# A gated MLP as nine equal Strassen products instead of three wide and twelve narrow ones

## The chip, the cores and the metric

The kernel runs on one core of one Trainium2 chip. The metric is device microseconds from launch to the last output byte, median of the runs. A core has a matrix engine (PE, TensorE, whose weight loads are listed as PEld), a vector engine (DVE), an activation engine (ACT), GpSimd (POOL) and a queue engine (SP) that issues most of the DMA transfers.

## The reference, cut to what matters

The program is a two-layer decoder trunk on 256 tokens of width 1024, float32 throughout: attention, a mixture of experts, the gated MLP of this case, and a second mixture of experts. Each of the four adds its result to `ALPHA * x` and normalises. The gated MLP is:

```
z = gelu(x @ w_in + b_in)              # x 256x1024, w_in 1024x6144
u, v = split(z, 2)                     # 256x3072 each
v = layer_norm(v, ln_v_g, ln_v_b)      # over all 3072 columns
mixed = tril(w_s)[g] @ v[chunk, :, g]  + b_s[g]   # 8 groups of 384 columns; chunks of 128 tokens
h = (u * mixed) @ w_out                # w_out 3072x1024
x = layer_norm(ALPHA * x + h)
```

The 256 tokens make two chunks of 128 rows, called row tile 0 and 1 below.

## The kernel before, in words

All weights pass through a ring of 24 buffers of 1 MB in SBUF, each 128 partitions by 2048 floats (`slot`, `drop`, L68 to L76). `piece` (L78) takes a buffer and issues its load on SP's queue. SP works through its loads in order; a load starts when its buffer has been released, so transfers run ahead of the compute as far as the ring has free buffers. The ring also holds activations. The order of instructions on each engine is drawn up when the program is built, by a planner that follows the order of the code but takes a later instruction of the same engine first when, by its own reckoning, the earlier one's inputs are not there yet. On the chip each engine then works through that list in order.

Strassen's scheme (in Winograd's form) multiplies two matrices that are cut into 2x2 blocks with seven block products instead of eight, at the price of sums of blocks made beforehand and of results. Here a block product with 512 inner values is four matmul calls of 128 inner values each (`prod`, `prod_u`), and every float32 matmul call appears in the trace as two MATMUL instructions.

`gmlp` (L362) has these stages.

- **v**, L404 to L442: three passes of 1024 columns. The tokens are the stationary operand, 512 weight columns move; seven products of four matmuls each. The block sums of the weights are `t1`, `t2` and two sums in place: three on DVE and one, `b12 = b22 - b12`, on POOL (L422). The sums of x (`sums_x`, L354) are made once. DVE adds bias and partial results, ACT applies gelu, DVE takes the statistics of the layer norm.
- **u**, L483 to L519: twelve passes of 256 columns. Here the weights are the stationary operand and 128 tokens move (`prod_u`, L476), so that u comes out transposed, with columns in partitions. The sums of the weights are on DVE (`sums_w`, L448).
- **mix**, L525 to L548, inside the same loop: per 128 columns, `w_s` times the normalised v (L538), then bias, affine and the product with u on DVE (L534 to L546).
- **output projection**, `proj` (L471): 24 steps of 128 inner values, each with two row tiles times two halves of 512 columns, into four PSUM banks kept open through the whole loop. Its matmuls are placed between the products of the next u pass (`step`, L492).
- **close** (L211, called at L558 and L561): adds `ALPHA * x`, normalises each row tile and transposes it for the router of the second mixture of experts.

Before `gmlp`, at the end of the first mixture of experts, loads for its biases and `w_s` are issued from ACT's queue, behind the last block's Silu (`end = mid(pa, h)`, L904; `after(end)`, L369 and L388). PE's fillers `keep_warm(2)` (L903 and L920) multiply a matrix of ones. After `gmlp`, `moe(1, ...)` starts with the dense expert (`dense_up`, L593), the router (L578), and the first gather (L705).

Of the kernel before, what the change touches and what calls it, by code (L numbers as in the profile page):

```python
# [19 lines left out]
P = 128  # L20
# [29 lines left out]
def trunk(ctx: ExitStack, tc: tile.TileContext, t, out):  # L50
# [15 lines left out]
    held = {}  # L66

    def slot(late=False):  # L68
        i = idle.pop() if late else idle.popleft()
        s = ring.tile([P, 2048], F32, tag=f"s{i}", name=f"s{i}")  # L70
        held[id(s)] = (i, s)
        return s

    def drop(*slots):
        for s in slots:
            idle.append(held.pop(id(s))[0])  # L76
# [158 lines left out]

    def attention(xT_slot, x):
        xT = by_k(xT_slot)
        with tc.tile_pool(name="att", bufs=1) as att, tc.tile_pool(name="att2", bufs=2) as att2:
# [76 lines left out]
            for g in range(3):  # L315
                qkv_g = qkv(g, w)
                if g == 0:
                    nc.sync.dma_start(x, t["x"].rearrange("(a p) d -> p a d", p=P))
                w = [piece(t["wqkv"][3 * (g + 1) + i]) for i in range(3)]
                for c in range(2):  # L320
                    heads(g, c, *qkv_g, psY, "Y")
# [32 lines left out]
    def sums_x(xT, s):  # L354
        x11, x12, x21, x22 = (xT[:, 4 * h:4 * h + 4, a * P:(a + 1) * P] for a in range(2) for h in range(2))
# [3 lines left out]
        nc.vector.tensor_tensor(s[:, 2], x11, x21, op=OP.subtract)  # L359


    def gmlp(xT_slot, x, end):  # L362
        xT = by_k(xT_slot)
        with tc.tile_pool(name="gm", bufs=1) as gm, tc.tile_pool(name="gm2", bufs=2) as gm2:
            cols = gm.tile([P, 3, NCH], F32, name="cols")
            wb_slot = slot()
            wb = wb_slot.rearrange("p (i g q) -> p i g q", i=2, g=GG)
            ws, bs = wb[:, 0], wb[:, 1]
            with after(end):  # L369
                nc.scalar.dma_start(cols, t["gcols"])  # L370
                nc.scalar.dma_start(ws, t["gw_s"])
                nc.scalar.dma_start(bs, row_bc(t["gb_s"], GG * P).rearrange("p (g q) -> p g q", g=GG))
            nc.gpsimd.affine_select(out=ws, in_=ws, compare_op=OP.is_ge, fill=0.0, base=0,
                                    pattern=[[0, GG], [1, P]], channel_multiplier=-1)
            scr = gm.tile([P, 4 * T], F32, name="scr")
            b_slot = slot()
            s_slot = slot()
            sx = s_slot.rearrange("p (s k t) -> p s k t", s=4, k=4)
            x11, x12, x21, x22 = (xT[:, 4 * h:4 * h + 4, a * P:(a + 1) * P] for a in range(2) for h in range(2))
            s1, s2, s3, s4 = (sx[:, i] for i in range(4))  # L380
            v_slots, vt = [], []
            st = gm.tile([P, NT, 6, 6], F32, name="vst")

            def pair_load(p):
                w = [piece(t["wv"][4 * p + i]) for i in range(4)]
                bv = [b_slot[:, (2 * p + i) % 4 * 512:(2 * p + i) % 4 * 512 + 512] for i in range(2)]
                for i in range(2):
                    with after(end):  # L388
                        nc.scalar.dma_start(bv[i], row_bc(t["gb_v"][(2 * p + i) * 512:(2 * p + i + 1) * 512], 512))
                return w, bv  # L390

            def prod(ps, xs, w, start, stop):
                for k in range(4):
                    nc.tensor.matmul(ps, xs[:, k, :], by_k4(w)[:, k, :], start=start and k == 0, stop=stop and k == 3,  # L394
                                     skip_group_check=True)

            def add(o, i, j):
                nc.vector.tensor_tensor(o, i, j, op=OP.add)

            def sub(o, i, j, eng=nc.vector):  # L400
                eng.tensor_tensor(o, i, j, op=OP.subtract)  # L401


            ld = pair_load(0)  # L404
            for p in range(3):
                (b11, b21, b12, b22), bv = ld
                v_slots.append(slot(p > 0))
                vt.append(by_a(v_slots[-1]))
                c = [[vt[p][:, a, n * 512:(n + 1) * 512] for n in range(2)] for a in range(2)]
                t1, t2 = slot(True), slot(True)  # L410
                px, py, pz = bank(psA, "A"), bank(psY, "Y"), bank(psY, "Y")
                sub(t1, b12, b11)
                sub(t2, b22, t1)
                prod(px, x11, b11, True, False)
                prod(py, x12, b21, True, True)
                add(c[0][0], px, bv[0])
                if p == 0:
                    sums_x(xT, sx)
                add(c[0][0], c[0][0], py)
                prod(px, s2, t2, False, False)  # L420
                add(c[0][1], px, bv[1])
                sub(b12, b22, b12, nc.gpsimd)  # L422
                prod(pz, s1, t1, True, False)
                p5 = scr[:, p % 2 * 512:p % 2 * 512 + 512]
                nc.scalar.copy(p5, pz)
                drop(b11)
                sub(b21, b21, t2)
                prod(px, s3, b12, False, False)
                add(c[1][1], px, bv[1])
                prod(pz, s4, b22, False, True)  # L430
                add(c[0][1], c[0][1], pz)
                add(c[1][1], c[1][1], p5)
                nc.scalar.activation(vt[p][:, 0, :], vt[p][:, 0, :], AF.Gelu)
                if p < 2:
                    ld = pair_load(p + 1)
                prod(px, x22, b21, False, True)
                add(c[1][0], px, bv[0])
                nc.scalar.activation(vt[p][:, 1, :], vt[p][:, 1, :], AF.Gelu)
                for a in range(NT):
                    for n in range(2):  # L440
                        nc.vector.bn_stats(st[:, a, 2 * p + n, :], c[a][n])
                drop(b21, b12, b22, t1, t2)  # L442

            t_slots = [slot(True), slot(True)]
            wu = [piece(t["wu"][0])]


            def sums_w(q):  # L448
                w = by_k(wu[q])
                s = t_slots[q % 2].rearrange("p (s k n) -> p s k n", s=4, k=4)  # L450
                b11, b12, b21, b22 = (w[:, 4 * h:4 * h + 4, j * P:(j + 1) * P] for h in range(2) for j in range(2))
                sub(s[:, 0], b12, b11)
                sub(s[:, 1], b22, s[:, 0])
                sub(s[:, 2], b22, b12)
                sub(s[:, 3], b21, s[:, 1])
                return b11, b21, b22, s

            sw = sums_w(0)
            nrm = []
            for a in range(NT):  # L460
                mv = small.tile([P, 2], F32, tag="mv", name="mv")
                nc.vector.bn_aggr(mv, st[:, a])
                nrm.append((mv, rsqrt(mv[:, 1:2])))
            for cb in range(6):
                for a in range(NT):
                    v = vt[cb // 2][:, a, (cb % 2) * 512:(cb % 2) * 512 + 512]
                    nc.vector.tensor_scalar(v, v, nrm[a][0][:, 0:1], nrm[a][1], op0=OP.subtract, op1=OP.mult)

            acc = [[bank(psY, "Y") for _ in range(2)] for _ in range(NT)]

            def proj(a, i, mx, wo):  # L471
                for h in range(2):
                    nc.tensor.matmul(acc[a][h], mx[:, a, :], by_c(wo)[:, i % 2, h * 512:(h + 1) * 512],  # L473
                                     start=(i == 0), stop=(i == NCH - 1))

            def prod_u(ps, w, xs, start, stop):  # L476
                for k in range(4):
                    nc.tensor.matmul(ps, w[:, k, :], xs[:, k, :], start=start and k == 0, stop=stop and k == 3,  # L478
                                     skip_group_check=True)


            done = []
            for q in range(NCH // 2):  # L483
                wo = piece(t["wout"][q])
                if q + 1 < NCH // 2:
                    wu.append(piece(t["wu"][q + 1]))
                b11, b21, b22, tw = sw
                fill = [(a, *d) for d in done[-2:] for a in range(NT)]
                if q == NCH // 2 - 1:
                    fill = [f for f in fill if f[0] == 0]  # L490

                def step():  # L492
                    if fill:
                        proj(*fill.pop(0))

                px, py, pz = (bank(psA, "A")[:, :P], bank(psB, "B")[:, :P], bank(psB, "B")[:, :P])
                u = [gm2.tile([P, T], F32, tag="u", name="u", bufs=3) for _ in range(2)]
                p5 = gm.tile([P, P], F32, tag="p5", name="p5")
                prod_u(px, b11, x11, True, False)
# [493 lines left out]
```

## Time and profile before

| what | value |
|---|---|
| median of 3 runs (lowest to highest) | 1350.84 us (1348.72 to 1351.52) |
| the profiled execution: time of its own | 1352.34 us |
| its span, first to last instruction | 1350.6 us |
| PE busy | 1234.4 us (91%), 6706 matmuls |
| DVE busy | 346.9 us (26%) |
| ACT busy | 133.5 us (10%) |
| DMA | 469.05 MB, mean 347 GB/s |

The page cuts the span into 40 slices of 33.8 us. The gated MLP lies in slices 19 to 26 of them (618.9 to 874.1 us). In the two mixtures of experts the DMA line stands at 9 and some 420 GB/s; in the gated MLP the DMA moves 149 to 277 GB/s in most slices. "Busy" of PE is the time in which at least one matmul is in flight; the rate of matmuls is read from the distance between their starts.

### The profile page before, as it was taken

The page shows a single profiled execution, that of the slowest core. Times are in us where ns is not written, and L with a number is a line of the kernel's source. Part 1 is how long each engine was busy: PE and PEld are TensorE (multiplying, and loading weights), DVE is VectorE, ACT ScalarE, POOL GpSimd, SP SyncE. Part 2 cuts the span into 40 slices and gives each one's busy share as a digit, 9 for nine tenths or more (in the row PEclk, how much of TensorE's full clock was granted, in tenths as well). Part 3 has the DMA queues.
Part 4 walks back from the last instruction along what each step waited for, and adds up shares of the span by engine and source line. Part 5 has one row for each costly group of instructions (what it writes and reads, how often), then busy time and mean ns, then how long its engine had stood idle before and what let it go on. Part 6 is the DMA issues. An engine that isn't in the chain of part 4 may idle for free. (4 is left out here: it accounts for less than half of the span.)

```text
span 1350.6 us, 17128 instructions
## 1 busy us (share of the span) xinstructions
PE 1234.4 (91%) x6706; PEld 620.0 (46%) x6706; DVE 346.9 (26%) x827; ACT 133.5 (10%) x318; POOL 30.1 (2%) x48
## 2 busy tenths in 40 slices
PE   8999999998898888887999999999998888988886
PEld 7776554433333333322457777655433333433331
DVE  1322531111111111016775433442111111111112
ACT  1321100000000000001111111110000000000000
POOL 2000000000000000001200000000000000000000
PEclk9999999999999999998999999989999999999999
DMA  9946389999999999999764445649999999999996
GB/s 362 420 151 228 125 329 421 421 421 421 421 421 419 422 420 421 420 385 404 277 224 149 156 159 184 263 151 421 420 420 422 421 420 420 420 422 421 420 420 245
DMA packets 71016, 469.05 MB, mean 347 GB/s; under 512 B 8080, under 2 KB 8080, under 8 KB 16784
## 3 DMA queue, kind: packets, MB, share of 16 engines
q1 hardware_dynamic: 69056, 464.55, 84.7%
q10 hardware_dynamic: 1872, 3.32, 0.8%
q8 instruction: 56, 0.92, 0.3%
q14 instruction: 32, 0.26, 0.1%
HBM read 466.79 MB, written 1.05 MB: 346 GB/s over the span
## 5 line engine op out<-in xcount | busy, mean ns | idle before, releaser
L746 PE MATMUL A<-s,s 128*32 128x512 f32 x2048 | 307.4, 607 | 36.1 <-DMA s<-in_w 27.6
L843 PE MATMUL B<-s,s 128*32 128x512 f32 x1024 | 185.3, 601 | 28.0 <-DVE s L838 14.4
L746 PEld LDWEIGHTS A<-s,s 128*32 128x32 f32 x2048 | 71.3, 111 | 219.8 <-issue 160.1
L705 PEld LDWEIGHTS B<-s,s 128*128 128x128 f32 x1024 | 121.5, 195 | 45.7 <-issue 27.3
L103 DVE COPY s<-B 128x512 f32<-128x512 f32 x64 | 44.3, 692 | 367.1 <-PE B L705 208.6
L705 PE MATMUL B<-s,s 128*128 128x128 f32 x1024 | 131.3, 283 | 0.0
L855 PE MATMUL Y<-s 128*128 128x512 f32 x256 | 118.9, 606 | 2.4 <-ACT s L105 1.5
L843 PEld LDWEIGHTS B<-s,s 128*32 128x32 f32 x1024 | 45.2, 109 | 147.8 <-issue 78.3
L473 PE MATMUL Y<-s,scr 128*128 128x512 f32 x192 | 89.5, 593 | 0.0
L105 ACT COPY s<-B 128x512 f32<-128x512 f32 x64 | 37.5, 585 | 525.9 <-PE B L843 265.7
L855 PEld LDWEIGHTS Y<-s 128*128 128x128 f32 x256 | 45.8, 189 | 77.0 <-issue 60.9
L262 PE MATMUL A<-s,s 128*128 128x256 f32 x256 | 64.0, 396 | 5.4 <-DMA s<-in_wqkv 5.4
L478 PEld LDWEIGHTS A<-s,s 128*128 128x128 f32 x384 | 49.5, 192 | 16.1 <-issue 12.9
L262 PEld LDWEIGHTS A<-s,s 128*128 128x128 f32 x256 | 48.8, 199 | 14.9 <-issue 8.7
L755 DVE TENSOR_TENSOR s<-s,A 128x256 f32<-128x256 f32 x32 | 13.5, 420 | 158.5 <-ACT s L754 158.5
L478 PE MATMUL A<-s,s 128*128 128x128 f32 x384 | 51.6, 276 | 0.4 <-ACT u L501 0.4
L394 PE MATMUL A<-s,s 128*128 128x512 f32 x96 | 46.1, 629 | 3.5 <-DVE s L401 3.4
L691 DVE TENSOR_TENSOR s<-iota_t,sm 128x256 f32<-128x256 f32 (+1 forms) x56 | 21.1, 413 | 102.0 <-PE A L746 102.0
L401 DVE TENSOR_TENSOR s<-s,s 128x512 f32<-128x512 f32 (+1 forms) x33 | 40.8, 1238 | 24.0 <-PE A L478 20.9
L473 PEld LDWEIGHTS Y<-s,scr 128*128 128x128 f32 x192 | 33.2, 191 | 25.3 <-issue 25.1
L754 ACT ACTIVATE s<-A 128x256 f32<-128x256 f32 x32 | 12.3, 383 | 305.1 <-PE A L746 289.5
L478 PE MATMUL B<-s,s 128*128 128x128 f32 x288 | 38.0, 275 | 0.0
(209 smaller groups left out, 852.0 us busy)
## 6 DMA issues: line engine op xcount, KB each, us to landing
s<-in_w SPq DMA_DIRECT2D x372, 1024.0 KB, 19.8
s<-in_w SPq DMA_DIRECT2D x24, 512.0 KB, 12.1
s<-in_wv SPq DMA_DIRECT2D x12, 1024.0 KB, 14.7
s<-in_wu SPq DMA_DIRECT2D x12, 1024.0 KB, 4.9
s<-in_wout SPq DMA_DIRECT2D x12, 1024.0 KB, 5.2
s<-in_wqkv SPq DMA_DIRECT2D x11, 1024.0 KB, 19.4
s<-in_wo SPq DMA_DIRECT2D x4, 1024.0 KB, 20.5
s<-in_ln_g SPq DMA_DIRECT2D x4, 512.0 KB, 8.2
```

Of the source, the lines that this page charges most:

```text
L103: nc.vector.tensor_copy(o, i)
L105: nc.scalar.copy(o, i)
L262: nc.tensor.matmul(ps[:, :T], wt[:, kc, c * P:(c + 1) * P], xT[:, kc, :], start=(kc == 0), stop=(kc == KC - 1))
L394: nc.tensor.matmul(ps, xs[:, k, :], by_k4(w)[:, k, :], start=start and k == 0, stop=stop and k == 3, skip_group_check=True)
L401: eng.tensor_tensor(o, i, j, op=OP.subtract)
L473: nc.tensor.matmul(acc[a][h], mx[:, a, :], by_c(wo)[:, i % 2, h * 512:(h + 1) * 512], start=(i == 0), stop=(i == NCH - 1))
L478: nc.tensor.matmul(ps, w[:, k, :], xs[:, k, :], start=start and k == 0, stop=stop and k == 3, skip_group_check=True)
L691: nc.vector.tensor_tensor(oh[i][:, :, :n], over(at, n), s.to_broadcast([P, NT, n]), op=OP.is_equal)
L705: nc.tensor.matmul(ps[:, k * P:(k + 1) * P], x[:, a, kc * P:(kc + 1) * P], oh[2][:, a, :], start=(a == 0), stop=(a == NT - 1))
L746: nc.tensor.matmul(pa[32 * j:32 * j + 32, :], xg[:, kc, 32 * j:32 * j + 32], by_k4(w[min(j, len(w) - 1)])[:, k, :], start=(kc == 0), stop= ...
L843: nc.tensor.matmul(py[32 * j:32 * j + 32, :], hT[:, c, 32 * j:32 * j + 32], by_c(w[min(j, len(w) - 1)])[:, c, n * 512:(n + 1) * 512], star ...
L855: nc.tensor.matmul(acc[a][n], gT[:, a * P:(a + 1) * P], ye[:, n * 512:(n + 1) * 512], start=first, stop=last, skip_group_check=extra)
```

## The change

All three matrix multiplications of `gmlp` become the same routine, `seven`: a 256x1024 by 1024x1024 multiplication by seven block products, tokens stationary, 512 columns moving. It runs nine times: three for v, three for u, three for the output projection (1024 inner values each). u is thus made with tokens in rows; so v is mixed in rows too, u times the mix is transposed on PE (`turn`), and the transposed result is the stationary operand of the projection, whose sums of blocks are made anew for each third (`sums_x` in `turn`). The projection's results are added to x by DVE, product by product (`put` in `out`).

- All sums of weight blocks are on DVE, each cut in two instructions of 128x1024 (`sub`). `t1` and `t2` lie in two buffers that all nine share.
- The layer norm's scale goes into `w_s` (`wsa`, one copy per row tile); mean and gain go into v (`centre`); the layer norm's bias, the row sums of `w_s` and `b_s` make one row per 1024 columns. These rows are needed along the free dimension: `make_rows`, in the attention, turns the columns on PE and writes them to a DRAM buffer, from which ACT's queue loads them, spread over the partitions (`in_bias`, `ln_rows`).
- The mixing, the transposes and `centre` are handed to `seven` as `fill`, at given places between its products.
- The ring becomes one tile of 24 x 2048; `double` takes two neighbouring buffers, in which the four pieces of a third lie (`four`), and a third is loaded one third ahead (`ahead`).
- At the end of a mixture of experts, `end` is now the last ACT copy of `down` instead of the Silu, and the second `keep_warm(2)` is put behind the last matmul of `back`.

```diff
-    def slot(late=False):
-        i = idle.pop() if late else idle.popleft()
-        s = ring.tile([P, 2048], F32, tag=f"s{i}", name=f"s{i}")
+    room = ring.tile([P, RING * 2048], F32, name="s")
+    def take(i, n=1):
+        s = room[:, i * 2048:(i + n) * 2048]
...
+    def sub(o, i, j):
+        for k in (slice(0, 2), slice(2, 4)):
+            nc.vector.tensor_tensor(o[:, k], i[:, k], j[:, k], op=OP.subtract)
+    def seven(A, S, B, t, p5, put, done, fill={}):
...
+        px, py, pz, pw = bank(psA, "A"), bank(psY, "Y"), bank(psY, "Y"), bank(psY, "Y")
...
+        sub(t1, b12, b11)
+        sub(t2, b22, t1)
+        prod(px, x11, b11, True, False)
+        prod(py, x12, b21, True, True)
+        put(0, 0, px)
+        put(0, 0, py)
+        at(0)
+        prod(pz, S[:, 0], t1, True, False)
+        nc.scalar.copy(p5, pz)
+        sub(b21, b21, t2)
+        at(1)
+        prod(px, S[:, 1], t2, False, False)
+        put(0, 1, px)
+        sub(b12, b22, b12)
+        at(2)
+        prod(pz, S[:, 3], b22, False, True)
+        put(0, 1, pz)
+        done(0)
+        at(3)
+        prod(pw, x22, b21, True, True)
+        put(1, 0, pw)
+        at(4)
+        prod(px, S[:, 2], b12, False, True)
+        put(1, 1, px)
+        put(1, 1, p5)
+        put(1, 0, px)
+        done(1)
...
-                sub(b12, b22, b12, nc.gpsimd)
...
-            for q in range(NCH // 2):
...
-                prod_u(px, b11, x11, True, False)
...
+            half_in(0, {0: [lambda: sums_x(A, S)]})
+            half_in(1, {2: [ws_rows]})
+            ln_rows(0)
+            half_in(2)
...
+                nc.vector.tensor_scalar(wsa[:, a], ws, rsqrt(mv[:, 1:2]), None, op0=OP.mult)
...
+            def centre(i):
+                v = by_a(vt[i])
+                for a in range(NT):
+                    nc.vector.scalar_tensor_tensor(v[:, a], v[:, a], mean[a], g_slot[:, :1024],
+                                                   op0=OP.subtract, op1=OP.mult)
+                for g, c, e in parts(i):
+                    b = g_slot[:, 1024 + c:1024 + e]
+                    nc.vector.tensor_scalar(b, b, rs[:, g:g + 1], bs8[:, g:g + 1], op0=OP.mult, op1=OP.add)
+            def mix(i):
...
+                for a in range(NT):
+                    for j in range(2):
+                        ps = bank(psB, "B")
+                        for g, c, e in parts(i):
+                            if c // 512 == j:
+                                nc.tensor.matmul(ps[:, c - 512 * j:e - 512 * j], wsa[:, a, g], v[:, a, c:e],
+                                                 start=True, stop=True)
+                        nc.vector.tensor_add(v[:, a, sl], ps, g_slot[:, 1024 + 512 * j:1536 + 512 * j])
+                        nc.vector.tensor_mul(u[:, a, sl], u[:, a, sl], v[:, a, sl])
+                drop(vt[i])
+                if i < 2:
+                    ln_rows(i + 1)
+            def turn(i):
+                got, half = transposer(by_a(ut[i]))
+                for a in range(NT):
+                    for h in range(2):
+                        half(a, h)
+                m = halves(by_k(got[0]))
+                s = slot(True, True)
+                sums_x(m, by_s(s))
...
+            centre(0)
+            half_in(3)
+            half_in(4, {0: [lambda: mix(0)], 1: [lambda: centre(1)], 3: [lambda: turn(0)]})
+            out(0, lambda a: None, {0: [lambda: mix(1)], 1: [lambda: centre(2)]})
+            half_in(5, {3: [lambda: turn(1)]})
...
+            out(1, lambda a: None, {0: [lambda: mix(2)], 3: [lambda: turn(2)]})
...
+            out(2, close_tile)
...
-            end = mid(pa, h)
+            mid(pa, h)
...
-            down(h, hT, ye, w2, gT, last=True)
+            end, done = down(h, hT, ye, w2, gT, last=True)
...
-                keep_warm(2)
+                with after(done):
+                    keep_warm(2)
```

## Rows read from the trace of the kernel before

**Rows 1.** Windows by stage: v, the u loop, and the second experts' main part.

```profile
core 0: us, PE busy (x) PEld busy (x) DVE busy (x) ACT busy (x) POOL busy (x), PEclk, DMA share, GB/s
618.90:700.90 82.00, 78.08 (x184) 34.53 (x185) 59.97 (x61) 10.57 (x13) 14.42 (x4) 0.96 0.73 290
640.00:700.90 60.90, 60.88 (x140) 26.62 (x139) 41.07 (x43) 7.74 (x8) 9.03 (x2) 0.98 0.64 244
700.90:874.10 173.20, 172.22 (x978) 124.91 (x977) 75.44 (x178) 27.79 (x81) 2.19 (x3) 1.00 0.51 184
910.00:1350.60 440.60, 386.18 (x2280) 159.34 (x2272) 68.65 (x155) 24.86 (x48) 1.10 (x2) 0.99 0.98 407
```

**Rows 2.** Windows of 5 us: a wait in v, and after the gated MLP.

```profile
630.00:635.00 5.00, 2.35 (x6) 0.76 (x4) 5.00 (x1) 0.59 (x1) 3.57 (x1) 1.00 1.00 416
635.00:640.00 5.00, 4.23 (x5) 1.85 (x6) 3.52 (x3) 0.00 (x0) 0.00 (x0) 0.50 1.02 424
...
885.00:890.00 5.00, 5.00 (x17) 3.68 (x17) 1.97 (x13) 0.22 (x1) 0.00 (x0) 0.50 0.00 0
```

**Rows 3.** Timeline of PE in the u loop: start, us in flight, instruction, count.

```profile
753.93 1.06 PE L478 MATMUL B<-s,s 128*128 128x128 f32 x8
754.82 1.88 PE L473 MATMUL Y<-s,scr 128*128 128x512 f32 x4
756.54 1.05 PE L478 MATMUL A<-s,s 128*128 128x128 f32 x8
```

**Rows 4.** Timeline of PE where v starts; in brackets idle before, and its releaser.

```profile
618.96 1.29 PE L230 MATMUL B<-ident,s 128*128 128x128 f32 x8 [2.43 <-DVE s L206]
620.31 3.70 PE L394 MATMUL A<-s,s 128*128 128x512 f32 x8
...
628.65 3.70 PE L394 MATMUL Y<-s,s 128*128 128x512 f32 x8 [0.33 <-DVE s L401]
635.77 6.71 PE L394 MATMUL A<-s,s 128*128 128x512 f32 x8 [3.42 <-DVE s L401]
```

**Rows 5.** Timeline of POOL, and of DVE, in the same stretch.

```profile
628.73 4.84 POOL L401 TENSOR_TENSOR s<-s,s 128x2048 f32<-128x2048 f32 x1 [6.92 <-DVE s L401]
...
626.31 2.28 DVE L401 TENSOR_TENSOR s<-s,s 128x2048 f32<-128x2048 f32 x1
...
629.71 6.00 DVE L401 TENSOR_TENSOR s<-s,s 128x2048 f32<-128x2048 f32 x1
```

**Rows 6.** Groups of DVE and ACT by form: count, busy us, mean ns.

```profile
L401 DVE TENSOR_TENSOR s<-s,s 128x512 f32<-128x512 f32 x24 | 16.6, 691 | 21.3 <-PE A L478 20.9
...
L398 DVE TENSOR_TENSOR s<-A,s 128x512 f32<-128x512 f32 x12 | 8.2, 683 | 9.0 <-PE A L394 9.0
...
L205 DVE SCALAR_TENSOR_TENSOR s<-s,mv,s 128x512 f32<-128x512 f32 x4 | 2.8, 745 | 0.0
...
L231 ACT COPY s<-B 128x512 f32<-128x512 f32 x12 | 6.6, 588 | 53.0 <-PE B L230 41.5 <-DVE s L215 11.5
```

**Rows 7.** Timeline of DVE inside the third pass of v.

```profile
688.01 1.28 DVE L401 TENSOR_TENSOR s<-s 128x512 f32<-128x512 f32 x2
```

**Rows 8.** Timeline of all engines at the end of the gated MLP.

```profile
873.91 1.28 DVE L215 SCALAR_TENSOR_TENSOR s<-s,Y 128x512 f32<-128x512 f32 x2
874.00 1.04 PE L230 MATMUL B<-ident,s 128*128 128x128 f32 x8
874.24 0.35 ACTq L570 DMA_DIRECT2D wr<-in_wr  x1
...
882.37 5.41 PE L578 MATMUL B<-wr,s 128*128 128x72 f32 x32 [1.26 <-DMA wr<-in_wr]
...
899.23 0.94 PE L705 MATMUL B<-s,s 128*128 128x128 f32 x7
```

**Rows 9.** Timeline of ACT at the end of the first experts.

```profile
613.91 0.58 ACT L105 COPY s<-B 128x512 f32<-128x512 f32 x1 [14.87 <-PE B L843]
```

**Rows 10.** DMA issues by line: size, median us from issue to landing.

```profile
s<-in_gb_v ACTq DMA_DIRECT2D x6, 256.0 KB, 7.9
```

More of the change, by code (lines that the diff above doesn't have):

```diff
@@ L444, in gmlp @@
[L444 to L456, printed above, removed]
@@ L469, in gmlp @@
[L469 to L479, printed above, removed]
@@ new lines, in half_in, with done @@
+            def half_in(i, fill={}):
+                ahead(i)
+                w, B, bias = loaded[i]
+                to = vt if i < 3 else ut
+                d = slot(True, True)
+                to[i % 3] = d
+                d = by_a(d)
+                def done(a):
+                    nc.scalar.activation(d[:, a], d[:, a], AF.Gelu)
+                    if i < 3:
+                        for n in range(2):
+                            nc.vector.bn_stats(st[:, a, 2 * i + n, :], d[:, a, n * 512:n * 512 + 512])
+                p5 = gm2.tile([P, 512], F32, tag="p5", name="p5")
+                seven(A, S, B, t_of(i), p5, put_in(d, bias), done, fill)
+                drop(*w)
@@ new lines, in gmlp, with ws_rows @@
+            rs = gm.tile([P, GG], F32, name="rs")
+            def ws_rows():
+                ps = bank(psB, "B")
+                for g in range(GG):
+                    nc.tensor.matmul(ps[:, g:g + 1], ws[:, g, :], ones[:, 0:1], start=True, stop=True)
+                nc.scalar.copy(rs, ps[:, :GG])
+            half_in(0, {0: [lambda: sums_x(A, S)]})
+            half_in(1, {2: [ws_rows]})
+            ln_rows(0)
+            half_in(2)
+            wsa_slot = slot(True, True)
+            wsa = wsa_slot.rearrange("p (a g q) -> p a g q", a=NT, g=GG)
@@ new lines, in gmlp, with out, put @@
+            mixed = {}
+            def turn(i):
[6 more added lines that the diff above has]
+                sums_x(m, by_s(s))
+                mixed[i] = (got[0], s, m)
+                drop(ut[i])
+            def out(i, done, fill={}):
+                ahead(6 + i)
+                w, B, _ = loaded[6 + i]
+                m, s, M = mixed[i]
+                first = set() if i == 0 else {(a, n) for a in range(NT) for n in range(2)}
+                def put(a, n, ps):
+                    c = x[:, a, n * 512:n * 512 + 512]
+                    if (a, n) in first:
+                        nc.vector.tensor_tensor(c, c, ps, op=OP.add)
+                    else:
+                        first.add((a, n))
+                        nc.vector.scalar_tensor_tensor(c, c, ALPHA, ps, op0=OP.mult, op1=OP.add)
+                p5 = gm2.tile([P, 512], F32, tag="p5", name="p5")
+                seven(M, by_s(s), B, t_of(6 + i), p5, put, done, fill)
+                drop(*w, m, s)
@@ L554, in gmlp, with close_tile @@
-            for l in late[2:]:
-                proj(0, *l)
-            for l in late[:-1]:
-                proj(1, *l)
-            close(x, 0, acc, gb, half)
-            proj(1, *late[-1])
-            drop(late[0][2], late[2][2])
-            close(x, 1, acc, gb, half)
-            drop(gb)
+            def close_tile(a):
+                s = [x[:, a, h * 512:(h + 1) * 512] for h in range(2)]
+                st = small.tile([P, 2, 6], F32, tag="bns", name="bns")
+                stats(s, st)
+                norm(x, a, s, st, gb, half)
```

274 lines of the change are left out of this document (120 added, 154 removed).

## The prediction

> **What bounds the kernel now.** I read the windows by stage first. In the second experts the DMA engines are busy 0.98 of the time at 407 GB/s; there the loads set the time. In the gated MLP they run at 290 and 184 GB/s while PE has matmuls in flight for 78.1 of 82.0 us (v) and 172.2 of 173.2 us (the u loop) [rows 1]; there PE sets it, and DVE is busy for 75.4 of the 173.2 us. Behind the gated MLP stand 5 us in which the DMA moves nothing [rows 2]: the ring is full and waits for the first expert blocks to be consumed. So what PE gains in the gated MLP moves the second experts forward whole, as long as the ring is full again when they begin.
>
> A full busy row is not a rate. The distance between starts is: eight matmuls of 128 columns take 753.93 to 754.82, 0.111 us each, and four of 512 columns 754.82 to 756.54, 0.430 us each [rows 3]. A column costs 0.87 ns in the narrow form and 0.84 ns in the wide one. The reader should see here that widening alone is worth 4%, not a factor.
>
> The third view is the start of v. PE waits 3.42 us for DVE, and the next eight matmuls take 6.71 us in flight instead of 3.70 [rows 4]: the clock is granted at 0.50 (1.2 GHz) between 635 and 640 us [rows 2]. DVE was late because one subtraction of 2048 columns took 6.00 us, beside a POOL subtraction of 4.84 us that began 1 us before; the same subtraction alone takes 2.28 us [rows 5].
>
> **Part by part, PE.** All counts are from the code, two instructions a call.
> - u: 12 x 7 x 4 x 2 = 672 at 0.111 = 74.6 us become 3 x 7 x 4 x 2 = 168 at 0.430 = 72.2 us: -2.4.
> - Projection: 24 x 4 x 2 = 192 at 0.430 = 82.6 us become 168, 72.2 us: -10.4. This is the one large term: eight block products become seven.
> - Mix: 96 of 128 columns (10.7 us) become 48 of 128 to 384 columns, 12,288 columns in all as before, 10.4 us: -0.3. The row sums of `w_s`, 16 at 0.111 = 1.8 us, leave this stage; 16 of one column stand in v instead, put at 1.5 us.
> - Transposes of u times mix: 48. Eight are in flight for 1.04 us in all [rows 8], some 0.115 each: +5.5.
>
> So the u loop and projection, 700.9 to 874.0 = 173.1 us, of which the instructions above are 169.7 and waits 3.4, become 160.3 us plus waits.
>
> **The waits.** The trace has no 1024-column subtraction; 512 columns take 0.69 us [rows 6] and 2048 take 2.28 [rows 5], so I take the point between, 1.22. One `seven` costs DVE eight of those and eight `put` at 0.68: 15.2 us, against 56 x 0.430 = 24.1 us of PE. Six of them after v: 91. To this come mixing, 24 at 0.69 = 16.6; `centre`, six of 1024 columns at no more than two of 0.745 [rows 6] each and twelve of 128 to 384 columns, some 13 in all; `sums_x` 12 at 0.69 = 8.3; `wsa` two at no more than 1.22 = 2.4; the closing of row tile 0, 4.8. That is 136 us of DVE under 160 us of PE: 85%, where it was 44%. It fits, but no longer loosely.
>
> If DVE took its work strictly as the code has it, the place to look is the fourth `seven`: after the last product of v come three `put` (2.1), gelu and statistics (2.5), mean and power (1.3), `wsa` (2.1 to 2.4), `centre(0)` (4.2, a third of the 13), and then `t1` (2.4), ready 14.6 us after that product, while PE needs `t1` after two products, 6.9 us: a wait of 7.7. By the same walk `half_in(4)` waits 2.8, `out(0)` 5.0 (`centre(2)` stands behind the load of `ln_rows(2)`, which is issued only after `mix(1)` and lands some 7.9 us later [rows 10], and `b12` queues behind it), `half_in(5)` 0.6, `out(1)` 1.6. The upper end is thus 17.7 us, the lower end 0. The planner does not keep that order: the subtractions of `sums_w(0)`, which stand behind the third v pass in the code, ran at 688.0 us in the middle of it [rows 7]. `t1` and `t2` can likewise be made as soon as products 3 and 4 of the `seven` before have read them. What I leave standing is mixing, where the third of four banks waits for DVE to empty the first (1 us, three times), the transposes, where ACT's copy of a bank (0.588 [rows 6]) is slower than its four transposes (0.6 us, three times), and a remainder: I take 5 us, against 3.4 now: +1.6. With the -9.4 of the instructions this stage gives -7.8.
>
> **v.** 620.3 to 700.9 = 80.6 us: 168 at 0.430 = 72.2, eight transposes 0.9, so 7.5 of waits, of which 3.4 are the wait on DVE and 3.0 the half clock [rows 4]. Without POOL's subtraction DVE does, from its last normalising step near 623.8, `t1` and `t2` (4.9), two `put` (1.4) and `sums_x` (2.8), 9.1 us, to 632.9. PE has two products until 628.2; the third needs the first of the sums and `t1`, which leaves 0 to 2.5 us. I take 2.5 and no clock loss, plus 1.1 of the other waits and 1.5 for the row sums: 78.2, that is -2.4. Bounds: -4.9 (no wait), +1.5 (wait and half clock as now).
>
> **The end.** Three additions follow the last product instead of two (873.91, 1.28 us for two [rows 8]): +0.7. The router waits 1.26 us for `wr` already, whose load was issued at 874.24, right after the last matmul [rows 8]; its memory comes from the closed pools, where now `p5` is read by one of those last additions: +1.0 (0 to 2). Together +1.7.
>
> **What I cost at nothing, or nearly.** `make_rows`: two transposes and two copies in the attention, +0.3. Biases and `w_s` are now issued behind the ACT copy that ends at 614.5 [rows 9]; with 7.9 us to land [rows 10] they are there at 622.4, and the first `put` is due when the first product is done, 620.3 + 8 x 0.43 = 623.8. The cover is 1.4 us; a load of twice the size that took 12 us would cost some 3. `keep_warm` moves into PE's 2.43 us wait before 618.96 [rows 4]: 0, between -1 and +1. Loads in the gated MLP: 4 MB in 24 us is 175 GB/s, as now.
>
> **The sum.** -7.8 - 2.4 + 1.7 + 0.3 = -8.2 us. The profiled execution took 1352.3 us (span 1350.6), so 1344.1; it lies 1.5 us over the median of the runs, so 1342.6 against 1350.84.
>
> **Rivals.**
> - *DVE's order binds.* Waits of 17.7 us instead of 5, and two of them over the 3.42 us after which the clock fell [rows 2, 4], so 3.0 more each: 18.7 us worse than my sum, 1361.3, slower than before. It decides from 13.2 us of waits on. For it: 85% load and fills that hang on loads. Against: rows 7. Chance 0.15.
> - *The clock falls at each `turn`.* There PE does 16 transposes and waits for ACT between them, 2.4 us without another product if the planner puts none there; three times 3.0 us gives 1351.6, no change. For it: at 885 to 890 us the clock is at 0.50, 11 us after PE's last long run of wide matmuls and behind such transposes [rows 2, 8]. Against: eight transposes at 618.96 [rows 4] were followed by 1.00 at 630 to 635 [rows 2]. Chance 0.08. The Trainium skill (TensorE: Matmul & The Clock Gate, Part 4: PE-mode transpose) says that transposes do not count as PE work for the clock in the same way; by that this rival would be the likelier one, and the rows at hand speak for both.
> - *DVE hides wholly.* Waits of 1 us and a clean start of v (-4.9): 1336.1. For it: PE has matmuls in flight for 60.88 of 60.90 us in the later part of v [rows 1], with the same routine in its older form. Chance 0.20.
> - *The gain is given back by the loads.* Nine buffers (four weights, two of the transposed product, `t1`, `t2`, the norm's) come free only about the last product; 9.4 MB at the 416 GB/s of rows 2's first window fill them in 22.6 us, and the first gather of the experts starts 25.2 us after the end (899.23 - 874.0 [rows 8]). The margin is 2.6 us; were the loads held up by 11 us, the time would stay near 1350.8. Against: the DMA stands idle there now. Chance 0.07.
>
> **How the numbers follow.** The forecast holds 0.50, with a range of its own of 1337 to 1349 (waits from 0 to 11 us). A measurement of this kernel can tell 0.2%, 2.7 us, from no change. Faster: 0.48 of the forecast and the 0.20 of the hidden DVE, 0.68. Same: 0.05 of the clock rival, 0.06 of the loads, 0.01 of the forecast, 0.12. Slower: 0.15, 0.03 of the clock, 0.01 of the loads and 0.01 of the forecast, 0.20. The range goes from 1333 (no waits, all small terms at their low ends) to 1356 (waits of 18 us without the clock), which leaves out the worst of DVE's rival.
>
> **What would show it.** In the profile after: starts of wide matmuls 0.430 us apart in u and projection; 168 of them for each of the three; the stage from the first product to the last 238 to 244 us instead of 253.7. DVE near 85% behind v, with `t1` of the fourth `seven` made before that `seven` begins. No half clock at 635 us. I am wrong if PE's idle time behind v sums to over 13 us, if the clock falls inside the stage, or if the DMA runs without a pause at the start of the second experts and the gated MLP's gain does not reach the end.

## The result, and the profile after

The changed kernel takes 1334.01 us (median of 4 runs, 1332.11 to 1334.46) against 1351.16 for the kernel before (1348.72 to 1351.52): by the medians 17.1 us less. The kernel before was timed again beside every experiment; its 45 runs lie between 1345.78 and 1354.41 us, with a median of 1350.1, and against that the change is 16.1 us. The ratio on record, 0.9881 with a 95% interval of 0.9869 to 0.9894, says the same: 16.1 us, 14.3 to 17.7. The forecast was 8.2 us less, half of it. The direction held, and the range of 1333 to 1356 by 1 us at its low end, which had been put there for no waits and all small terms at their lowest; the forecast's own range of 1337 to 1349 missed.

The profiled executions have spans of 1350.6 and 1332.1 us, 18.5 apart; the stages below add up to that. The first product of u begins in the middle of a row of PE's timeline, after eight matmuls that are still v's, at 692.52 + 8 x 0.430 = 695.96 us:

```profile
692.52 7.03 PE L408 MATMUL A<-s 128*128 128x512 f32 x16
```

| stage, from the starts of PE's instructions | before | after | difference | forecast |
|---|---|---|---|---|
| start of v | 620.31 | 619.89 | -0.4 | +0.3 |
| v, first product to first product of u | 80.6 | 76.1 | -4.6 | -2.4 |
| u and projection, to the first dense matmul of the second experts (before: to the end of the projection, 874.0) | 173.1 | 160.9 | -12.2 | -7.8 |
| from there to the router | 8.4 | 9.9 | +1.5 | +1.7 |
| router to the first gather | 16.9 | 14.3 | -2.6 | 0 |
| first gather to the end of the span | 451.4 | 451.1 | -0.2 | 0 |

The windows of the changed kernel, answering to [rows 1] and [rows 2] (columns as there):

```profile
619.80:699.50 79.70, 78.87 (x202) 36.16 (x202) 65.61 (x84) 11.34 (x15) 3.08 (x3) 1.00 0.77 308
699.50:856.80 157.30, 157.30 (x433) 75.80 (x432) 114.44 (x149) 17.16 (x26) 2.38 (x2) 1.00 0.55 213
...
865.00:870.00 5.00, 3.29 (x22) 3.32 (x23) 0.00 (x0) 0.89 (x1) 0.00 (x0) 0.83 1.02 419
870.00:875.00 5.00, 5.00 (x16) 3.45 (x16) 2.38 (x17) 0.96 (x2) 0.00 (x0) 0.50 0.31 129
```

PE has a matmul in flight in all of the 157.3 us, at a clock of 1.00; DVE is busy for 114.4 us of them, 73%, where the forecast said 85%. The half clock of 635 to 640 us is gone, that behind the gated MLP is still there (now 870 to 875). PE's waits, summed by releaser from 610 to 880 us (total us, times, longest):

```profile
PE B L656 <- DMA wr<-in_wr: 1.9, 1, 1.9
PE B L245 <- DVE s L221: 1.5, 2, 0.8
PE Y L935 <- ACT s L924: 0.8, 1, 0.8
```

None of the three lies between 625.5 us and the end of the projection: the first is the router, the second the transposes of the input at 618.6 and 624.4 us, the third the end of the first experts. The start of v, PE's timeline, answering to [rows 4]:

```profile
619.89 3.70 PE L408 MATMUL A<-s 128*128 128x512 f32 x8
624.37 1.29 PE L245 MATMUL B<-ident,s 128*128 128x128 f32 x8 [0.79 <-DVE s L221]
625.50 7.03 PE L408 MATMUL Y<-s 128*128 128x512 f32 x16
632.37 3.60 PE L408 MATMUL A<-s 128*128 128x512 f32 x8
```

The third product follows the second inside the row of 16, without a pause: the wait of 3.42 us is gone. Later, where the mixing (L583) and the turns (L245) stand between the products:

```profile
726.86 1.90 PE L583 MATMUL B<-s 128*128 128x384 f32 x8
728.59 1.88 PE L408 MATMUL Y<-s 128*128 128x512 f32 x4
730.30 1.90 PE L583 MATMUL B<-s 128*128 128x384 f32 x8
...
740.62 1.04 PE L245 MATMUL B<-ident,s 128*128 128x128 f32 x8
741.49 1.02 PE L408 MATMUL Y<-s 128*128 128x512 f32 x2
742.35 1.04 PE L245 MATMUL B<-ident,s 128*128 128x128 f32 x8
```

A row of eight is two banks in both cases. The planner has put four or two matmuls of a product between the second bank and the third, where the code has none. Eight transposes take 0.87 us from start to start, 0.109 each. DVE, answering to [rows 6] and [rows 7]: first the group of the subtractions in the gated MLP (count, busy us, mean ns, idle before), then its timeline at the turn from v to u.

```profile
L404 DVE TENSOR_TENSOR s<-s 128x1024 f32<-128x1024 f32 x72 | 85.2, 1216 | 5.8 <-PE Y L408 5.8
```

```profile
679.60 7.01 DVE L404 TENSOR_TENSOR s<-s 128x1024 f32<-128x1024 f32 x6
...
703.30 1.22 DVE L404 TENSOR_TENSOR s<-s 128x1024 f32<-128x1024 f32 x1
704.43 0.68 DVE L512 TENSOR_TENSOR s<-A,s 128x512 f32<-128x512 f32 x1
705.03 1.21 DVE L404 TENSOR_TENSOR s<-s 128x1024 f32<-128x1024 f32 x1
```

Six subtractions run in one block in the middle of the third set of v. Counted over v, 30 of the 72 begin before 695.96 us, where v's own three sets have 24: the other six, three weight sums in halves, belong to the fourth set and are made before it begins. One takes 1.22 us as estimated, but the next instruction starts 1.13 us after it (703.30 to 704.43), and the one behind a `put` of 0.68 us after 0.60 (704.43 to 705.03). The end, first by all engines, then by PE, answering to [rows 8]:

```profile
858.23 0.69 DVE L613 TENSOR_TENSOR s<-s,p 128x512 f32<-128x512 f32 x1
...
858.95 0.34 ACTq L648 DMA_DIRECT2D wr<-in_wr  x1
```

```profile
856.83 6.17 PE L678 MATMUL Y<-s 128*128 128x512 f32 x14
...
863.80 1.02 PE L678 MATMUL Y<-s 128*128 128x512 f32 x2
866.71 5.67 PE L656 MATMUL B<-wr,s 128*128 128x72 f32 x32 [1.88 <-DMA wr<-in_wr]
...
880.97 3.73 PE L783 MATMUL B<-s 128*128 128x128 f32 x32
```

The router's weights are issued 0.03 us after the last addition, that of `p5`, ends (858.92), and the router waits 1.88 us for them.

### The profile page after: what moved, and what is told of

Same layout as the page of the kernel before. It is cut to its first block, busy times and chain, and to the rows that moved or that the text cites. A ratio compares the mean times of both kernels' runs of the same rounds, so it can differ in the third digit from the quotient of the medians.

```text
span 1332.1 us, 16031 instructions
## 1 busy us (share of the span) xinstructions
PE 1221.2 (92%) x6180; PEld 572.9 (43%) x6180; DVE 393.6 (30%) x827; ACT 125.9 (9%) x265; POOL 17.8 (1%) x45
## 5 line engine op out<-in xcount | busy, mean ns | idle before, releaser
L824 PE MATMUL A<-s 128*32 128x512 f32 x2048 | 304.9, 600 | 36.1 <-DMA s<-in_w 26.9
L920 PE MATMUL B<-s 128*32 128x512 f32 x1024 | 187.5, 598 | 29.2 <-DVE s L915 14.9
L824 PEld LDWEIGHTS A<-s 128*32 128x32 f32 x2048 | 70.7, 110 | 217.2 <-issue 157.5
L783 PEld LDWEIGHTS B<-s 128*128 128x128 f32 x1024 | 121.7, 195 | 46.4 <-issue 26.9
L783 PE MATMUL B<-s 128*128 128x128 f32 x1024 | 131.6, 284 | 0.0
L408 PE MATMUL Y<-s 128*128 128x512 f32 x288 | 128.8, 592 | 0.0
L935 PE MATMUL Y<-s 128*128 128x512 f32 x256 | 118.9, 606 | 1.6 <-ACT s L924 1.5
L408 PE MATMUL A<-s 128*128 128x512 f32 x216 | 96.1, 593 | 0.0
L404 DVE TENSOR_TENSOR s<-s 128x1024 f32<-128x1024 f32 x72 | 85.2, 1216 | 5.8 <-PE Y L408 5.8
L295 PE MATMUL A<-s 128*128 128x256 f32 x256 | 64.4, 398 | 5.5 <-DMA s<-in_wqkv 5.5
L408 PEld LDWEIGHTS A<-s 128*128 128x128 f32 x216 | 40.9, 190 | 51.0 <-issue 48.8
L295 PEld LDWEIGHTS A<-s 128*128 128x128 f32 x256 | 49.2, 200 | 15.2 <-issue 8.9
## 6 DMA issues: line engine op xcount, KB each, us to landing
s<-in_w SPq DMA_DIRECT2D x24, 512.0 KB, 10.4
```

The source lines that it names most:

```text
L295: nc.tensor.matmul(ps[:, :T], wt[:, kc, c * P:(c + 1) * P], xT[:, kc, :], start=(kc == 0), stop=(kc == KC - 1))
L404: nc.vector.tensor_tensor(o[:, k], i[:, k], j[:, k], op=OP.subtract)
L408: nc.tensor.matmul(ps, xs[:, k, :], w[:, k], start=start and k == 0, stop=stop and k == 3, skip_group_check=True)
L783: nc.tensor.matmul(ps[:, k * P:(k + 1) * P], x[:, a, kc * P:(kc + 1) * P], oh[2][:, a, :], start=(a == 0), stop=(a == NT - 1))
L824: nc.tensor.matmul(pa[32 * j:32 * j + 32, :], xg[:, kc, 32 * j:32 * j + 32], by_k4(w[min(j, len(w) - 1)])[:, k, :], start=(kc == 0), stop= ...
L920: nc.tensor.matmul(py[32 * j:32 * j + 32, :], hT[:, c, 32 * j:32 * j + 32], by_c(w[min(j, len(w) - 1)])[:, c, n * 512:(n + 1) * 512], star ...
```

## The experiments

Theory: the gain is the instructions removed (seven block products for eight, wide u), plus PE's waits, which vanish because the planner lets DVE make weight sums early. Rival: the waits never depended on DVE's order. Each kernel is the changed one with one edit, unless said otherwise; differences in us are to its 1334.0, and the ratios are to the kernel before, as above; "stage" is the first product of v to the end of the projection, 236.9 us in the changed kernel (619.89 to 856.83).

**DVE in the order of the code.** Every DVE instruction of the gated MLP is chained behind the one before it in the code (one helper, so all of them have one line, L395).

```diff
+            def call(*a, **k):
+                with after(InOrder.last):
+                    InOrder.last = getattr(nc.vector, name)(*a, **k)
```

> The changed kernel, with every DVE instruction of the gated MLP (up to the last closing) chained to run in the order of the code; nothing else changed. Theory (the planner's order hid DVE): the walk of the prediction comes true, PE waits about 17 us behind v, most of it (7.7 us) for t1 of the fourth product set, and the clock falls once or twice at 3 us each: 1351 to 1358 us, PE idle over 12 us in the stage. Rival (DVE simply has room, order is no matter): PE waits under 3 us, 1334 to 1337 us.

1337.26 us (1334.86 to 1337.9), ratio 0.9901 [0.9874, 0.9929]; stage 245.2, 8.3 more. The theory's number failed, but its walk was right for DVE: DVE's timeline at the fourth set, then PE's, there and at the start of v.

```profile
712.47 4.62 DVE L395 TENSOR_TENSOR s<-s 128x1024 f32<-128x1024 f32 x4
```

```profile
632.07 6.75 PE L421 MATMUL Y<-s 128*128 128x512 f32 x8 [0.69 <-DVE s L395]
...
706.46 3.60 PE L421 MATMUL A<-s 128*128 128x512 f32 x8
710.21 1.97 PE L596 MATMUL B<-s 128*128 128x384 f32 x8 [0.15 <-DVE s L395]
713.74 3.70 PE L421 MATMUL Y<-s 128*128 128x512 f32 x8 [1.56 <-DVE s L395]
```

`t1`, the first two of those four subtractions, is ready near 714.8, 14.3 us after the last product of v, against 14.6 in the walk. Yet PE waits 1.7 us there, not 7.7: its list puts in the first product of the next set (706.46) and half of `mix(0)` (710.21) before the third product. The other waits of the stage, leaving aside the one ahead of the input's transposes that the changed kernel has too, are 2.0 us, and a half clock at 632 us costs 3.1 (6.75 us for eight wide matmuls). The total grows by 3.3 us only: in the profiled execution the stage began 1.0 us earlier, and from its end to the first gather it took 21.1 us instead of 24.1, mainly since the clock did not fall behind the router's wait. So it is not DVE's order alone that hides DVE; PE's order does it too.

**PE in the order of the code.** The counterpart: products, row sums, mixing and turns are chained on PE (all at L398); DVE is free.

```diff
-            nc.tensor.matmul(ps, xs[:, k, :], w[:, k], ...
+            pe.matmul(ps, xs[:, k, :], w[:, k], ...
```

> The changed kernel, with the matmuls and transposes of the gated MLP (products, row sums, mixing, turns; not the closing transposes) held on PE in the order of the code; DVE stays free to take what is ready. It is the other half of the run with DVE in code order, and tries the 5 us of waits that the prediction left standing, since these supposed that PE stands at a late bank instead of taking a product whose inputs are there. Theory (the planner's order on PE is what took those waits away): three times some 1 us in the mixing, three times 0.6 us in the transposes and up to 1 us at the start, so 3 to 6 us of PE waits after 625 us, stage 240 to 243 us against 236.9, time 1337 to 1341 us. Rival (DVE's early work alone took them away; PE's order plays no part): waits under 1.5 us, stage under 238.5 us, time 1332 to 1336.

1338.26 us (1337.43 to 1338.93), 0.9918 [0.9898, 0.9938]; stage 242.1, 5.2 more. The theory holds. PE's waits, and one of each in its timeline:

```profile
PE B L398 <- DVE s L598: 2.3, 3, 0.8
...
PE B L398 <- ACT s L246: 1.6, 4, 0.8
```

```profile
727.60 2.00 PE L398 MATMUL B<-s 128*128 128x384 f32 x8 [0.79 <-DVE s L598]
...
797.34 0.66 PE L398 MATMUL B<-ident,s 128*128 128x128 f32 x4 [0.78 <-ACT s L246]
```

They are the places that the prediction named: the third bank of each mixing, and the transposes that wait for ACT's copy. By the starts of PE's instructions, the three mixings take 3.2 us more than their matmuls need and the three turns 2.6.

**DVE loaded more.** 4, 8 and 14 further subtractions in each of the last six sevens, into a buffer that nobody reads.

```diff
+        if spare is not None:
+            for _ in range(4):
+                nc.vector.tensor_tensor(spare, b22[:, 0:2], b22[:, 2:4], op=OP.subtract)
```

> The changed kernel with four more DVE subtractions of 128x1024 into an unused buffer in each of the six product sets behind v, some 28 us of DVE in all, so that DVE is busy for about 142 of 157 us there. Theory (DVE has that much room, since each engine's order is filled with whatever is ready): PE waits at most 3 us, 1334 to 1338 us. Rival (DVE is near the edge, each product set hangs on it): more than 10 us slower.

> The same with eight more per product set, some 56 us in all: DVE's work behind v comes to about 170 us against 160 of PE. Theory (DVE binds only when its sum passes PE's): the stage grows by 10 to 20 us and waits of PE on DVE show, 1344 to 1356 us. Rival (DVE never holds PE, its work can slip past the end): under 4 us slower.

> The changed kernel, with 14 more subtractions of 128x1024 on DVE in each of the last six sevens (84 at 1.14 us, as the run with eight of them had: 96 us). Between the first product of v and the last of the projection DVE was idle for 57 us of the changed kernel's 237. Theory (DVE's work is covered as long as its sum is below the stage's length, because both engines take whatever is ready): now the sum is 39 us over the stage, so the stage becomes 276 us or a little more, DVE is busy for 98% of it, PE waits in each seven, and the time is 1370 to 1378 us. Rival (the additions have so little behind them that even now they cost much less than their excess, since the bound is another): stage under 255 us, time under 1352.

With 4: 1332.22 us (1330.95 to 1338.78), 0.9886 [0.9852, 0.9919]; PE's waits between 640 and 862 us are 0.5 us, as the theory has it, and the time lies 1.8 us below its range. With 8: 1335.56 (1334.16 to 1337.02), 0.9892 [0.9871, 0.9913]. With 14: 1374.79 (1373.34 to 1375.85), slower than before, 1.0188 [1.0164, 1.0213]. One window, in the changed kernel, with 8 and with 14:

```profile
697.00:857.00 160.00, 160.00 (x439) 77.03 (x439) 115.82 (x151) 18.21 (x27) 2.38 (x2) 1.00 0.55 214
```

```profile
697.00:857.00 160.00, 159.79 (x434) 76.30 (x433) 158.95 (x193) 17.02 (x25) 2.57 (x3) 1.00 0.54 210
```

```profile
697.00:857.00 160.00, 144.24 (x389) 68.18 (x387) 159.56 (x187) 16.78 (x24) 1.46 (x1) 0.97 0.49 183
```

With 8, DVE is busy for 99% of the time and PE still loses 0.2 us: the theory's 1344 to 1356 fell, and its rival's under 4 us came true (1.55). DVE had been idle for 57 us of the gated MLP (14 in v, 43 behind it), and 48 subtractions at 1.14 us are 54.7. With 14 the additions (96 us) exceed that by 39, and the time rises by 40.8. The last projection product ends 24 us later than in the changed kernel, near 881; the rest shows behind it, where DVE works off additions until 899 us and the closing waits for it (4.74 and 4.27 us at PE's transposes). The stage's length (261.6) was not as expected, the total was. Up to 55 us of added work DVE was covered, and at 96 the excess was paid in full; between the two nothing was tried.

**POOL takes a quarter of the subtractions back.**

```diff
-        sub(b12, b22, b12)
+        sub(b12, b22, b12, nc.gpsimd)
```

> The changed kernel, with the fourth subtraction of weight blocks (b12 = b22 - b12, in two halves) on POOL again in all nine sevens, as it was in v before. Theory (DVE had 57 us of idle time, so taking 18 us from it gives nothing; what POOL does instead slows DVE's own subtractions beside it, 2.28 to 6.00 us in the kernel before): the start of v waits again for 2 to 4 us, elsewhere small waits or none; 1335 to 1340 us against 1334.0. Rival (POOL's work is now as well covered as DVE's): within 1 us of 1334.0, no wait over 1 us at the start of v. A gain of over 2 us would contradict both.

1345.19 us (1342.62 to 1346.33), 0.9961 [0.9944, 0.9979]: 11 us more, over both numbers. The wait at the start of v came as the theory has it; a second one of the same length, in the first mixing, was not expected. The groups of DVE and POOL in the gated MLP, and PE's two waits:

```profile
L404 DVE TENSOR_TENSOR s<-s 128x1024 f32<-128x1024 f32 x54 | 80.7, 1515 | 5.8 <-PE Y L408 5.8
...
L404 POOL TENSOR_TENSOR s<-s 128x1024 f32<-128x1024 f32 x18 | 51.6, 2869 | 145.8 <-DVE s L404 101.0 <-issue 22.0 <-DMA s<-in_w 21.4
```

```profile
635.20 4.97 PE L408 MATMUL A<-s 128*128 128x512 f32 x7 [3.28 <-DVE s L404]
...
738.33 3.67 PE L583 MATMUL B<-s 128*128 128x384 f32 x8 [3.21 <-DVE s L585]
```

Giving away 18 of 72 subtractions leaves DVE with 80.7 us instead of 85.2 for them, since those that run beside POOL stretch; other DVE instructions stretch too, and its whole busy time grows, from 180.9 (619 to 857 us) to 187.2 (619 to 866). Both waits are followed by a lower clock. This one line costs 11 us, most of what the whole change gains.

**Before, with that subtraction on DVE.** The same edit the other way, in the kernel before.

```diff
-                sub(b12, b22, b12, nc.gpsimd)
+                sub(b12, b22, b12)
```

> The kernel before, with the one subtraction of each v pass that POOL did put on DVE; nothing else changed. Theory (the slow start of v came from POOL and DVE reading side by side): the wait of 3.4 us and the half clock behind it go, 4 to 6 us faster than before, 1345 to 1347 us, and no subtraction of 2048 columns takes over 2.5 us. Rival (the start of v was freed by the later keep_warm or by the new order of products): under 1.5 us faster, the clock at 635 us still at 0.50.

1344.69 us (1342.15 to 1347.59), 0.9965 [0.9951, 0.9979]. That is 6.5 us less by the medians of its batch and 4.7 by the ratio; the theory holds. The stage v takes 75.6 us (618.92 to 694.48) instead of 80.6. The profiled executions differ by 9.4 us, more than that: 1.4 of it lies ahead of v and 2.9 between the router and the gather, and no run ties these to the edit. The wait of 3.42 us and the half clock behind it [rows 4] are gone; DVE's subtraction, then PE:

```profile
630.02 2.29 DVE L401 TENSOR_TENSOR s<-s,s 128x2048 f32<-128x2048 f32 x1
```

```profile
628.96 3.70 PE L394 MATMUL Y<-s,s 128*128 128x512 f32 x8 [0.33 <-DVE s L401]
632.49 3.60 PE L394 MATMUL A<-s,s 128*128 128x512 f32 x8
```

**The projection by eight products.**

```diff
-                sums_x(m, by_s(s))
...
-                seven(M, by_s(s), B, t_of(6 + i), p5, put, done, fill)
+                eight(M, B, put, done, fill)
```

> The changed kernel with the output projection by eight plain block products per third instead of seven, without its weight sums and without the sums of the transposed product; all else as changed. Theory (PE alone sets this stage): 3 x 8 more matmul instructions of 0.430 us, +10.3 us, 1344 to 1345 us, although DVE loses some 35 us of work. Rival (DVE's load holds PE back somewhere): less than 6 us slower, since DVE is freed, 1334 to 1340 us.

1339.22 us (1338.32 to 1340.78), 0.9923 [0.9896, 0.9951]. The stage is 10.2 us longer (619.72 to 866.88 = 247.2), as 24 instructions at 0.430 say. The total grows by only 5.2, since without the read of `p5` the router's weights load early (issued at 807.7 us); PE does not wait for them, and its clock stays up:

```profile
866.88 4.46 PE L690 MATMUL Y<-s 128*128 128x512 f32 x10
...
872.18 1.02 PE L690 MATMUL Y<-s 128*128 128x512 f32 x2
873.04 3.69 PE L668 MATMUL B<-wr,s 128*128 128x72 f32 x32
```

**The router's weights early.** They get memory of their own, beside the gated MLP's pools, and are issued before `out(1)`.

```diff
+            nc.scalar.dma_start(r1[:, :KC * 72], t["wr"][1].rearrange("p k e -> p (k e)"))
+            nc.scalar.dma_start(r1[:, KC * 72:], row_bc(t["br"][1], 72))
...
+    with tc.tile_pool(name="router", bufs=1) as router:
+        r1 = router.tile([P, KC * 72 + 72], F32, name="r1")
```

> The changed kernel with the router's weights of the second experts in a buffer of their own, loaded before the second third of the projection; nothing else changed. Theory (the router waits for that load, which waits for the last reader of p5, and PE's pause there halves the clock): the wait of 1.9 us before the router goes and the clock stays up for the router and the dense expert, 2 to 5 us faster, 1329 to 1332 us. Rival (the router would wait for row tile 1's transposes all the same): within 0.8 us of 1334.0.

1327.75 us (1326.45 to 1328.27), 0.9836 [0.9813, 0.9859]: the fastest version of all, 6.3 us under the changed kernel and a little under the number expected. Of the 6.8 us between the two profiled spans, 5.0 lie between the end of the projection and the gather, where the edit acts; 1.7 lie ahead of that, and no run ties them to the edit. PE:

```profile
863.00 3.69 PE L662 MATMUL B<-r,s 128*128 128x72 f32 x32
...
874.33 3.73 PE L789 MATMUL B<-s 128*128 128x128 f32 x32
```

No wait, 3.69 us instead of 5.67 for the router, and 11.3 instead of 14.3 us from it to the gather: the wait of 1.9 us cost another 2.9 in the lower clock behind it.

**u in narrow calls.** Each call of 512 columns in u becomes four of 128.

```diff
+        if len(w.shape) == 4:
+            for k in range(4):
+                for j in range(4):
+                    nc.tensor.matmul(ps[:, j * P:(j + 1) * P], xs[:, k, :], w[:, k, j // 2, ...
```

> The changed kernel, with the three sevens of u in calls of 128 columns instead of 512 (each call of 512 becomes four of 128, tokens still stationary; the computation is whole). Theory (a narrow column costs 0.111/128 us, a wide one 0.430/512, so u's 672 narrow instructions take 74.6 us against 72.2): stage +2.4 us, 239 to 241 us instead of 236.9; time 1335 to 1339. The earlier run of this edit, in which u lacked part of its sums, had +3.2. Rival (the width is what the change gained by): stage over 245 us.

1337.74 us (1334.75 to 1339.11), 0.9909 [0.9883, 0.9935]; stage 240.4 (618.13 to 858.58), 3.5 more, in the expected range; the width is not where most of the gain comes from. An earlier form of it, in which u lacked part of its partial sums, gave 1338.06 us and a stage of 240.1.

**`end` and the filler as before.**

```diff
-            end, done = down(h, hT, ye, w2, gT, last=True)
+            down(h, hT, ye, w2, gT, last=True)
```

> The changed kernel with the end of the first experts as before: loads for the gated MLP issued behind the Silu, the second keep_warm free for the planner to place. Theory (this edit only keeps the clock up at the start of v): 0 to 3 us slower, a lower clock between 615 and 625 us, the first eight wide matmuls of v over 4 us in flight. Rival (it costs nothing and gives nothing): within 1 us of 1334.0 and the clock at 1.00 there.

1334.17 us (1333.68 to 1335.25), 0.9884 [0.9864, 0.9904]: the rival holds. PE's wait ahead of v is 2.43 us again instead of 0.74, but the clock stays at 1.00 from 615 to 645 us, and the stage is 1.2 us shorter (620.34 to 856.08), mainly as the wait at the second transposes of the input is gone. That part of the change gains nothing.

## Why the prediction was right, and where its size was off

**Instructions: right.** 0.430 and 0.111 us from start to start [rows 3] priced the two gains near what the runs show: eight products for seven is 10.2 us (forecast 10.4), narrow u 3.5 at most (2.4). The stage behind v was to have 160.3 us of instructions; it took 160.9.

**The waits: the step that failed.** The prediction took 5 us: "mixing, where the third of four banks waits for DVE [...] (1 us, three times), the transposes [...] (0.6 us, three times), and a remainder". The runs show none. Held in code order, PE loses nearly this, 3.2 and 2.6 us, and the stage 5.2: the holes and their sizes were right, and that PE stands still in them was wrong. The row that the prediction used against the upper end [rows 7] says that the planner moves DVE's work forward; the prediction let the planner help DVE alone, and walked PE by the code. The planner does the same for PE: it fills these holes with matmuls of an open product. The 3.4 us of waits of the kernel before vanish as well: -9.4 - 3.4 = -12.8, of which 0.6 comes back beside the instructions, so -12.2 stands for -7.8.

**DVE's load: mis-sized, 85% for 73%.** The sum was made with durations (1.22, 0.68); instructions start 1.13 and 0.60 us apart, since neighbours overlap. By these distances the 136 us are some 123, and of those some 9 lie in v already: six subtractions of the fourth set (6 x 1.13), and the scale and centring of the first row tile (1.9). That leaves 114, which is what was measured. The runs with more subtractions show that the share did not matter up to 99%. The rival "DVE's order binds" had a chance of 0.15 for 17.7 us of waits and two falls of the clock; with DVE held in code order the stage grew by 8.3 us, and with DVE free nothing showed up to 55 us of added work.

**v: the low bound.** -4.6 against -2.4, bounds -4.9 to +1.5. The 2.5 us of waiting taken here did not come: `t1` is cut in two halves, the second half falls due only with the third product's third call, and DVE's distances are shorter than its durations. The half clock went as forecast, and the two runs that move one subtraction between POOL and DVE, one in each kernel, show the cause: POOL's subtraction beside DVE's.

**The end: right up to the router, incomplete behind it.** +1.5 for +1.7, and for the reason given: `wr` is held by the read of `p5`. What was not seen is that 16 dense matmuls now run before the router, where ten did, as the kernel before shows:

```profile
875.48 3.70 PE L600 MATMUL Y<-s,s 128*128 128x512 f32 x8 [0.44 <-ACT s L231]
...
880.09 1.02 PE L600 MATMUL Y<-s,s 128*128 128x512 f32 x2
```

Six times 0.430 is the 2.6 us that are missing between router and gather. The time ahead of the router, which the load of `wr` sets, is thus partly filled with work that stood behind it.

**The second experts:** the gain went through. DMA stands at 0.31 and 129 GB/s at 870 to 875 us, so it still pauses there, and the stretch from the first gather on takes 451.1 us as before (451.4): the rival of the loads is out.

**The clock at the turns: out.** In the run with PE in code order the second turn is 16 transposes in 3.25 us with two pauses and nothing beside them, and the clock from 760 to 800 us is 1.00:

```profile
760.00:800.00 40.00, 38.93 (x105) 18.05 (x104) 28.39 (x36) 4.27 (x7) 0.00 (x0) 1.00 0.34 122
```

By the Trainium skill (TensorE: Matmul & The Clock Gate, Part 4: PE-mode transpose) transposes do not count as PE work for the clock in the same way; no run here shows it, since every turn stands between matmuls of products.

**"DVE hides wholly" (1336.1) was the case that came true**, with a chance of 0.20: 1334.0, no waits behind v, and v 0.3 us above its low bound. That the walk through code order was carried out with care (14.3 us measured for 14.6) did not help: it described an order that neither engine follows.

## What to carry to other kernels

Where a planner orders the engines, walk none of them by the code: ask of each wait whether *any* engine involved has ready work to put there, and price it only if not. Here DVE stayed covered up to 99% and, with 39 us of work more than its idle time, cost the whole excess, so what counts is its sum of start-to-start distances against the stage, not a share that looks tight. Before moving work to POOL, compare DVE's durations with and without it beside; and look for small loads that wait for memory of a stage just ended, since the pause costs its length and, in eight of ten kernels here, the clock too.

## What had not been expected of the hardware

- The size of what POOL's subtractions of 128x1024 do beside DVE's: DVE's mean goes from 1216 to 1515 ns over all of its own, POOL's is 2869 ns.
- The clock behind the router's wait is not settled by the wait. PE pauses for `wr` for 1.5 to 2.6 us in ten kernels; in two (DVE in code order, and 4 more subtractions) the 32 matmuls that follow take 3.76 us, in the others 5.55 to 7.07. In the two kernels without that wait they take 3.69. In the kernel before they take 5.41 after 1.26 us, and 3.76 after 1.06 in that kernel with one line changed. What decides between the two was not found.
- What that fall costs: from the router to the gather, with 16 dense matmuls between them, 11.3 to 11.4 us in three kernels where the clock stayed at 1.00, 14.3 to 16.1 us in seven where it fell.
